# Parts of the k and q weights, made in the MLP and kept in memory, in a two-layer S5 and stick-breaking-attention decoder

## The chip, the cores and the metric

The kernel runs on one core of one Trainium2 chip. The metric is the device time of one execution in microseconds (us): the median of three runs of the kernel before is 2406.37 us (2405.84 to 2408.62). Besides these, one execution was taken with the hardware profiler; all rows below come from it.

## The reference

The model takes x of 1024 tokens by 1024 channels, in fp32. The part that matters here, in short:

```
x1 = LN(2^.5 * x  + S5_mixer(x) @ w_out)
h  = relu(x1 @ w1 + b1)^2               # MLP of layer 0, 4096 wide: first product
x2 = LN(2^.5 * x1 + h @ w2 + b2)        # second product
k, v = split(x2 @ w_kv);  q = x2 @ w_q  # 16 heads of 64
z[t,s] = q_t . k_s / 8,  s < t only
w[t,s] = sigmoid(z[t,s]) * prod_{s<j<t} (1 - sigmoid(z[t,j]))
x3 = LN(2^.5 * x2 + (w @ v) @ w_out2);  then the MLP of layer 1
```

## The kernel before

All products are made of three: every fp32 operand is kept as a high part (cast to the type `fp32r`) and a low part (the rest, in the same type), and a product is high x high + high x low + low x high. `split` (L121 to 123) makes the parts: a cast on ScalarE (`act.copy`, L122) and a subtract on VectorE (`dve.tensor_sub`, L123).

The stages stand one behind the other: the S5 layer and its projections to about 460 us; layer 0's first MLP product ("MLP up", `mlp_up`, names `m0...`) from 460 to 789; the second product (`Down`, names `d0...`) to about 1100; V (`VProject`) to 1194; the projections to K and Q and the attention, interleaved, to about 1640; then its output projection and layer 1's MLP.

**MLP up** is a Strassen-like scheme of 7 products per block of 256 hidden channels: 104 steps of one weight tile [128, 2, 512] (high and low) and 12 matmuls each, which accumulate in banks `m0A`, `m0C`, `m0B`. In each step a sum of raw weight tiles (`m0s...`, from the ring `x1ring`, loaded by SP at L843) is split into a slot (`sl`, 8 slots: 4 of pool `wa`, 4 of pool `wb`) two steps ahead of its use; ScalarE copies some banks out (`m0k...`, `keep`, L913), VectorE combines them (`m0h...`), GpSimd stores them to memory (`h_d`). Beside that `Down.ahead` prepares the next stage: 16 residual tiles (`d0ya`), one per five steps, are loaded by SP (L1041), scaled by ScalarE (L1043), given a bias by VectorE (L1044) and stored by SP (L1045). They live in pool `d0pf` with 4 buffers.

**K, Q and attention.** Per pair of heads p, `project_all` makes K and Q: 48 matmuls on each half, with a weight of [1024 x 128] stored as [128, 1024]. Its two halves (c = 0, 1) are loaded raw by SP (`r_k`, `r_q`, 256 KB, L133, a ring of 3 buffers) and split into slots of `wa` (`w_k`, `w_q`), one unit ahead of use; `VProject.run` does the first of them while V's last tiles are multiplied. `Step` is one block of 128 queries of one head: scores `pz` on TensorE, two sigmoids on ScalarE (`qq`, `be`, L1438 and 1439), a causal fill on GpSimd (L1441), a backward running product on VectorE (the scan, L1447) and a product (L1448), transposes on TensorE (`pt`, L1460), split of the transposed weights (`wTh`, `wTl`), the product with V (`po`, L1474), and a store to `o_d` by SP.

A scheduler orders the instructions of each engine from the order of the code and its own estimates; the engines run them in that order, and so does SP with its DMA issues. A tile of a pool is handed out again when its readers are done.

Of the kernel before, what the change touches and what calls it, by code (L numbers as in the profile page):

```python
# [16 lines left out]
P = 128  # L17
# [28 lines left out]
def trunk(ctx, tc, A, out):  # L46
# [32 lines left out]
    h_d = drp.tile([NP, 7, P, HF], F32, name="h_d")  # L79
    v_d = drp.tile([HEADS, KD, P, P], F32R, name="v_d")  # L80
    o_d = drp.tile([2, D, S], F32, name="o_d")

    class Act:

# [727 lines left out]
    def mlp_up(l, xo, y_tiles, w1, nm, ypool, tpool, tag, wb, uside, rest, down):  # L812
# [165 lines left out]
        for i in range(-LA, NSTEPS):  # L978
            if i + LA < NSTEPS:
                p, m = steps[i + LA]  # L980

                if (p, m) == (0, "M3"):
                    ready[0, "M6"] = operand(0, "M6")
                if (p, m) not in ready:
                    ready[p, m] = operand(p, m)
                if m == "M4" and p + 2 < NP:
                    load_raw(p + 2)
            if i < 0:
                continue
            p, m = steps[i]  # L990
            prod(p, m, ready.pop((p, m)))
            if later:
                later.pop(0)()
            if m == "M5" and p < EA:
                after(p, "M2")
            if m == "M4" and p + 1 < EA:
                keep(p + 1, "M1")
            down.ahead(i, NSTEPS, xo.ring)
            if (p, m) == (0, "M3"):
                continue  # L1000
            later += after(p, m)
            if (p, m) == (0, "M6"):
                after(0, "M3")
# [5 lines left out]
    class Down:  # L1009
# [6 lines left out]

        PARTS = ((0, 0), (1, 0), (0, 1), (1, 1))

        def __init__(self, l, nm, xd, wb, last, then=None):
            self.l, self.nm, self.xd, self.wb, self.last, self.then = l, nm, xd, wb, last, then  # L1020
            self.sl = Slots([wa] * 4 + [wb] * 4)
            self.raw, self.hraw, self.ready = {}, {}, {}
            self.st = ExitStack()
            self.units = [(c, m, p) for c in range(NP // CH) for m in self.ORDER for p in range(c * CH, (c + 1) * CH)]
# [6 lines left out]
        def tile(self, pl, nm_, tag):  # L1031
            return pl.tile([P, HF], F32, tag=tag, name=f"{self.nm}{nm_}")

        def ahead(self, i, n, ring):

            q, r = divmod(i - 12, 5)
            if 0 <= q < 16:
                xs = self.xd[tok(q // 2), half(q % 2)]
# [201 lines left out]
    def w1_ahead(l, w1):  # L1240
# [2 lines left out]
            w1.append(load_w(wa, w1_src(l, j // 2, 0, j % 2), f"m{l}1_{j}", HF)[0])  # L1243
        return one

    class VProject:


# [20 lines left out]
        def run(self, psA, trans, lns, sl):  # L1269
# [21 lines left out]
            for t in range(8):  # L1291
                mm(1, t)
                if t == 4:
                    self.wk0 = by_k(load_w(wa, A["w_k"][0], "k0"))


    with ExitStack() as ph:
        with ExitStack() as ph1:
# [47 lines left out]
                rest = proj_ln(ph2, flat(wo), lambda j: wsl.load(rows2(A["w_out"], j, half(1)), f"so1{j}"),  # L1346
                               gg, xo, x_d[0], y_load, A["lnmg"][0], A["lnmb"][0], "so", y_tiles, w1_ahead(0, w1))
            vpr = VProject()
            down = Down(0, "d0", x_d[0], wb, False, vpr)
            mlp_up(0, xo, y_tiles, w1, "m0", yst, bp, "gg", wb, "right", rest, down)  # L1350
        with ExitStack() as ph1:
            x2T = down.run(ph1)
# [17 lines left out]
    with ExitStack() as ph:  # L1370
# [5 lines left out]
        pso = mkpool(ph, "pso", 1, PSUM)  # L1376
        fl = lambda v_: v_.rearrange("p e t -> p (e t)")

        def load_p(nm, p):
            return by_k(load_w(wa, A[f"w_{nm}"][p], f"{nm}{p}"))  # L1380

        def project_all():


            seq = [(nm, p) for p in range(KD) for nm in "kq"]
            nxt = vpr.wk0
            for i, (nm, p) in enumerate(seq):
                w = nxt
                if i + 1 < len(seq):
                    nxt = load_p(*seq[i + 1])  # L1390
                hi, lo = hl = [qt.tile([P, S], F32R, tag=f"{nm}{y}", name=f"{nm}{y}{p}") for y in "hl"]
                for h in range(2):
                    ps = psj.tile([P, HF], F32, tag="j", name=f"pj{nm}{p}{h}")
                    for k in range(KD):
                        dense_fm({h: ps}, w, x2T, [k], (h,))
                        yield
                    split(hi[:, half(h)], lo[:, half(h)], ps)
                prs[p][nm] = hl
                if nm == "q":
                    stack(p, 0)  # L1400
                    yield
# [231 lines left out]
```

## Time and profile before

| | us |
|---|---|
| median of three runs | 2406.37 |
| profiled execution | 2409.81 |
| its span | 2408.1 |
| TensorE busy in the span | 2283.8 (95%) |
| VectorE busy | 1853.5 (77%) |
| ScalarE busy | 1220.4 (51%) |
| GpSimd busy | 409.1 (17%) |
| granted TensorE clock, mean | 0.981 of full |

The span runs from the first to the last instruction in the trace. In the rows PE is TensorE (PEld its weight loads), DVE VectorE, ACT ScalarE, POOL GpSimd, SP the queue that issues most DMAs. A row of a timeline gives the start, the length, the engine, the line, the operation, output<-input with shapes, and in brackets how long the engine had been idle before it and who released it. Idle time of an engine that nobody waits for costs nothing.

### The profile page before, as it was taken

The numbers are of one execution on the slowest core, as the hardware profiler recorded it, in microseconds if no ns is written. First come the engines' busy times: TensorE is split into PE (matmuls) and PEld (weight loads), VectorE is DVE, ScalarE is ACT, GpSimd is POOL, SyncE is SP. The second block draws the span as 40 slices with busy tenths as digits, with TensorE's granted clock in tenths as the row PEclk, the third lists the DMA queues.
The fourth block names the chain that finished last, engine by engine and source line by source line (L and its number), as shares of the span: only waits on it lengthen the run. The fifth ranks groups of instructions, "written<-read, shape, count | busy, mean of one in ns | idle before, by whom it ended". The sixth has DMA issues, their size and how long they took to land.

```text
span 2408.1 us, 32696 instructions
## 1 busy us (share of the span) xinstructions
PE 2283.8 (95%) x11072; PEld 1873.7 (78%) x11072; DVE 1853.5 (77%) x2899; ACT 1220.4 (51%) x2299; POOL 409.1 (17%) x704
## 2 busy tenths in 40 slices
PE   9987899999999999999999999888989999999996
PEld 7777787777888788888887888766777888788885
DVE  7899674886665787789169999896887666687888
ACT  5455441465555444445156777663356555444443
POOL 4000140012111000001144434341002111100001
PEclk9998999999999999999999999999999999999998
DMA  4221232376444845437655554555457343665432
GB/s 147 61 78 47 60 111 66 136 257 206 145 144 149 303 134 154 148 97 192 123 134 117 129 122 109 119 140 192 139 173 280 147 152 145 228 201 167 135 110 105
DMA packets 195160, 349.38 MB, mean 145 GB/s; under 512 B 23216, under 2 KB 66224, under 8 KB 194992
## 3 DMA queue, kind: packets, MB, share of 16 engines
q1 hardware_dynamic: 136112, 246.61, 32.4%
q0 software_dynamic: 58880, 100.69, 15.1%
q8 instruction: 87, 1.43, 0.3%
q14 instruction: 81, 0.66, 0.1%
HBM read 212.96 MB, written 100.66 MB: 130 GB/s over the span
## 4 chain that ended last, share of the span: by engine, by line
PE 65%; DVE 16%; issue 9%; DMA 4%; ACT 3%; POOL 2%; SPq 0%; POOLq 0%; DVEq 0%; ACTq 0%
PE d0M L1096 4%; PE d0M L1097 4%; PE d0M L1098 4%; PE d1M L1096 4%; PE d1M L1098 4%; PE d1M L1097 4%; DVE qq L1447 2%; PE m0A L832 2%; PE m0A L833 2%; PE m0A L834 2%; PE m1A L832 2%; PE m1A L834 2%; PE m1A L833 2%; DVE be L1448 2%; PE po L1474 2%
## 5 line engine op out<-in xcount | busy, mean ns | idle before, releaser
L1447 DVE TENSOR_TENSOR_SCAN qq<-qq 128x128 f32<-128x128 f32 (+7 forms) x128 | 173.7, 1359 | 12.1 <-POOL qq L1441 11.9
L1096 PE MATMUL d1M<-w_d12M,w_d1HM 128*128 128x512 f32 x448 | 175.7, 393 | 3.9 <-DVE d1y L1105 3.9
L1098 PE MATMUL d1M<-w_d12M,w_d1HM 128*128 128x512 f32 x448 | 175.9, 393 | 0.0
L1096 PE MATMUL d0M<-w_d02M,w_d0HM 128*128 128x512 f32 x448 | 174.7, 391 | 1.2 <-DVE d0y L1105 1.2
L1097 PE MATMUL d1M<-w_d12M,w_d1HM 128*128 128x512 f32 x448 | 175.4, 392 | 0.0
L1097 PE MATMUL d0M<-w_d02M,w_d0HM 128*128 128x512 f32 x448 | 174.8, 390 | 0.0
L1098 PE MATMUL d0M<-w_d02M,w_d0HM 128*128 128x512 f32 x448 | 174.6, 390 | 0.0
L122 ACT CAST w_d1HM<-d1hM 128x512 fp32r<-128x512 f32 x110 | 68.3, 621 | 170.1 <-PE d1M L1098 148.1
L122 ACT CAST w_d0HM<-d0hM 128x512 fp32r<-128x512 f32 x110 | 68.3, 621 | 169.0 <-PE d0M L1098 142.8
L122 ACT CAST wTh<-pt 128x512 fp32r<-128x512 f32 (+1 forms) x192 | 88.1, 486 | 84.1 <-PE pt L1460 83.6
L1460 PE MATMUL pt<-ident,be 128*128 128x128 f32 x576 | 91.2, 283 | 36.4 <-DVE wTl L123 28.0
L192 POOL TENSOR_TENSOR rsd<-ved,nhalf 128x1 f32<-128x1 f32 x16 | 16.2, 1014 | 621.1 <-DVE ved L190 612.9
L1460 PEld LDWEIGHTS pt<-ident,be 128*128 128x128 f32 x576 | 70.3, 144 | 62.1 <-issue 17.8
L123 DVE TENSOR_TENSOR w_d1HM<-d1hM,w_d1HM 128x512 fp32r<-128x512 f32 x110 | 75.8, 689 | 52.3 <-ACT w_d1HM L122 52.2
L123 DVE TENSOR_TENSOR w_d0HM<-d0hM,w_d0HM 128x512 fp32r<-128x512 f32 x110 | 75.9, 690 | 51.5 <-ACT w_d0HM L122 51.4
L123 DVE TENSOR_TENSOR wTl<-pt,wTh 128x512 fp32r<-128x512 f32 (+1 forms) x192 | 99.7, 545 | 11.5 <-ACT wTh L122 11.4
L1448 DVE TENSOR_TENSOR be<-be,qq 128x127 f32<-128x127 f32 (+7 forms) x128 | 99.4, 777 | 7.2 <-POOL be L1441 0.5
L1096 PEld LDWEIGHTS d1M<-w_d12M,w_d1HM 128*128 128x128 f32 x448 | 84.4, 188 | 24.1 <-ACT w_d12M L122 4.3
L1438 ACT ACTIVATE qq<-pz 128x512 f32<-128x512 f32 (+1 forms) x192 | 97.2, 507 | 10.9 <-DVE be L1448 5.3
L1096 PEld LDWEIGHTS d0M<-w_d02M,w_d0HM 128*128 128x128 f32 x448 | 84.1, 188 | 21.2 <-DVE d0y L1105 2.5
L1098 PEld LDWEIGHTS d1M<-w_d12M,w_d1HM 128*128 128x128 f32 x448 | 84.6, 189 | 18.4
L1097 PEld LDWEIGHTS d1M<-w_d12M,w_d1HM 128*128 128x128 f32 x448 | 84.6, 189 | 17.9
(480 smaller groups left out, 7084.5 us busy)
## 6 DMA issues: line engine op xcount, KB each, us to landing
d0hM<-h_d SPq DMA_DIRECT2D x110, 256.0 KB, 2.7
d1hM<-h_d SPq DMA_DIRECT2D x110, 256.0 KB, 2.7
x1ring<-in_w SPq DMA_DIRECT2D x70, 256.0 KB, 3.1
x3ring<-in_w SPq DMA_DIRECT2D x70, 256.0 KB, 3.2
h_d<-m0hs POOLq DMA_DIRECT2D x64, 256.0 KB, 2.8
h_d<-m1hs POOLq DMA_DIRECT2D x64, 256.0 KB, 2.8
d0r<-in_w SPq DMA_DIRECT2D x58, 256.0 KB, 3.7
d1r<-in_w SPq DMA_DIRECT2D x58, 256.0 KB, 3.3
```

Of the source, the lines that this page charges most:

```text
L122: act.copy(hi, src)
L123: dve.tensor_sub(lo, src, hi)
L832: pe.matmul(ps_, wh, xh[:, k], start=first and k == 0, stop=False, skip_group_check=True)
L833: pe.matmul(ps_, wh, xl[:, k], start=False, stop=False, skip_group_check=True)
L834: pe.matmul(ps_, wl, xh[:, k], start=False, stop=k == 3, skip_group_check=True)
L1096: pe.matmul(ps_, hh[:, tok(t)], wh, start=first, stop=False, skip_group_check=True)
L1097: pe.matmul(ps_, hh[:, tok(t)], wl, start=False, stop=False, skip_group_check=True)
L1098: pe.matmul(ps_, hl[:, tok(t)], wh, start=False, stop=last, skip_group_check=True)
L1438: act.activation(qq[:, s0:s1], pz, AF.Sigmoid, scale=-0.125)
L1447: dve.tensor_tensor_scan(out=rev, data0=rev, data1=rev, initial=1.0, op0=ALU.mult, op1=ALU.bypass)
L1448: dve.tensor_mul(be[:, 0:ns - 1], be[:, 0:ns - 1], qq[:, 1:ns])
L1460: pe.transpose(pt[:, b_], self.be[:, tok(s0 + b_)], ident)
```

## The change

A class `SplitKQ` is given to layer 0's `Down` and called in each step of MLP up. It loads each half of each w_k and w_q (32 raw tiles of 256 KB, two per five steps from step 12 on) into a buffer of `d0pf`, splits it four steps later into the next slot of MLP up, and stores the slot, 512 KB, to `kq_d` in memory. In V and in the attention `load_kq` loads the parts from there into the slots of `wa`, 512 KB each, without a split. Lines from 80 on move down by 1 to 31.

```diff
--- before.py
+++ after.py
@@ -79,6 +79,7 @@
     h_d = drp.tile([NP, 7, P, HF], F32, name="h_d")
     v_d = drp.tile([HEADS, KD, P, P], F32R, name="v_d")
     o_d = drp.tile([2, D, S], F32, name="o_d")
+    kq_d = drp.tile([2, KD, 2, P, 2, HF], F32, name="kq_d")
 
     class Act:
 
@@ -995,7 +996,7 @@
                 after(p, "M2")
             if m == "M4" and p + 1 < EA:
                 keep(p + 1, "M1")
-            down.ahead(i, NSTEPS, xo.ring)
+            down.ahead(i, NSTEPS, xo.ring, sl)
             if (p, m) == (0, "M3"):
                 continue
             later += after(p, m)
@@ -1016,7 +1017,8 @@
 
         PARTS = ((0, 0), (1, 0), (0, 1), (1, 1))
 
-        def __init__(self, l, nm, xd, wb, last, then=None):
+        def __init__(self, l, nm, xd, wb, last, then=None, job=None):
+            self.job = job
             self.l, self.nm, self.xd, self.wb, self.last, self.then = l, nm, xd, wb, last, then
             self.sl = Slots([wa] * 4 + [wb] * 4)
             self.raw, self.hraw, self.ready = {}, {}, {}
@@ -1031,8 +1033,10 @@
         def tile(self, pl, nm_, tag):
             return pl.tile([P, HF], F32, tag=tag, name=f"{self.nm}{nm_}")
 
-        def ahead(self, i, n, ring):
-
+        def ahead(self, i, n, ring, sl):
+
+            if self.job:
+                self.job.step(i, self.pf, sl)
             q, r = divmod(i - 12, 5)
             if 0 <= q < 16:
                 xs = self.xd[tok(q // 2), half(q % 2)]
@@ -1243,6 +1247,33 @@
             w1.append(load_w(wa, w1_src(l, j // 2, 0, j % 2), f"m{l}1_{j}", HF)[0])
         return one
 
+    class SplitKQ:
+
+
+        PARTS = [(y, p, c) for p in range(KD) for y in range(2) for c in range(2)]
+
+        def __init__(self):
+            self.raw = {}
+
+        def step(self, i, pl, sl):
+            for j, (y, p, c) in enumerate(self.PARTS):
+                i0 = 12 + 5 * j // 2
+                if i == i0:
+                    self.raw[j] = pl.tile([P, HF], F32, tag="p", name=f"kq{j}")
+                    dma.dma_start(self.raw[j], A[("w_k", "w_q")[y]][p][:, half(c)])
+                elif i == i0 + 4:
+                    t = sl.next().tile([P, 2, HF], F32R, tag="w", name=f"w_kq{j}")
+                    split(t[:, 0], t[:, 1], self.raw.pop(j))
+                    dma.dma_start(kq_d[y, p, c], t.bitcast(F32))
+
+    def load_kq(nm, p):
+        out = []
+        for c in range(2):
+            t = wa.tile([P, 2, HF], F32R, tag="w", name=f"w_{nm}{p}{c}")
+            dma.dma_start(t.bitcast(F32), kq_d["kq".index(nm), p, c])
+            out.append((t[:, 0], t[:, 1]))
+        return by_k(out)
+
     class VProject:
 
 
@@ -1291,7 +1322,7 @@
             for t in range(8):
                 mm(1, t)
                 if t == 4:
-                    self.wk0 = by_k(load_w(wa, A["w_k"][0], "k0"))
+                    self.wk0 = load_kq("k", 0)
 
 
     with ExitStack() as ph:
@@ -1346,7 +1377,7 @@
                 rest = proj_ln(ph2, flat(wo), lambda j: wsl.load(rows2(A["w_out"], j, half(1)), f"so1{j}"),
                                gg, xo, x_d[0], y_load, A["lnmg"][0], A["lnmb"][0], "so", y_tiles, w1_ahead(0, w1))
             vpr = VProject()
-            down = Down(0, "d0", x_d[0], wb, False, vpr)
+            down = Down(0, "d0", x_d[0], wb, False, vpr, SplitKQ())
             mlp_up(0, xo, y_tiles, w1, "m0", yst, bp, "gg", wb, "right", rest, down)
         with ExitStack() as ph1:
             x2T = down.run(ph1)
@@ -1376,9 +1407,6 @@
         pso = mkpool(ph, "pso", 1, PSUM)
         fl = lambda v_: v_.rearrange("p e t -> p (e t)")
 
-        def load_p(nm, p):
-            return by_k(load_w(wa, A[f"w_{nm}"][p], f"{nm}{p}"))
-
         def project_all():
 
 
@@ -1387,7 +1415,7 @@
             for i, (nm, p) in enumerate(seq):
                 w = nxt
                 if i + 1 < len(seq):
-                    nxt = load_p(*seq[i + 1])
+                    nxt = load_kq(*seq[i + 1])
                 hi, lo = hl = [qt.tile([P, S], F32R, tag=f"{nm}{y}", name=f"{nm}{y}{p}") for y in "hl"]
                 for h in range(2):
                     ps = psj.tile([P, HF], F32, tag="j", name=f"pj{nm}{p}{h}")
```

What the scheduler makes of it. First VectorE in MLP up, some 40 us into the stage. `d0ya` are the residual tiles, `w_m01M` the split weights, `m0s` and `m0h` sums of weights and of results. Before:

```order
L1044 TENSOR_TENSOR d0ya_4585<-d0ya_4585,d0b_4254 128x512
L1044 TENSOR_TENSOR d0ya_4714<-d0ya_4714,d0b_4254 128x512
L123 TENSOR_TENSOR w_m01M_4422<-m0sM_4420,w_m01M_4422 128x512
L1044 TENSOR_TENSOR d0ya_4833<-d0ya_4833,d0b_4254 128x512
L123 TENSOR_TENSOR w_m01M_4442<-x1ring,w_m01M_4442 128x512
L901 TENSOR_TENSOR m0sM_4465<-x1ring 128x512
L1044 TENSOR_TENSOR d0ya_4952<-d0ya_4952,d0b_4254 128x512
L929 TENSOR_TENSOR m0hA_4337<-m0kM_4335,m0C_4279 128x512
L123 TENSOR_TENSOR w_m01M_4467<-m0sM_4465,w_m01M_4467 128x512
L929 TENSOR_TENSOR m0hA_4358<-m0kM_4297,m0A_3972 128x512
```

Now, from the same place, and then some 30 rows on:

```order
L1048 TENSOR_TENSOR d0ya_4588<-d0ya_4588,d0b_4255 128x512
L124 TENSOR_TENSOR w_m01M_4423<-m0sM_4421,w_m01M_4423 128x512
L902 TENSOR_TENSOR m0sM_4466<-x1ring 128x512
L124 TENSOR_TENSOR w_m01M_4443<-x1ring,w_m01M_4443 128x512
L930 TENSOR_TENSOR m0hA_4338<-m0kM_4336,m0C_4280 128x512
L124 TENSOR_TENSOR w_m01M_4468<-m0sM_4466,w_m01M_4468 128x512
L930 TENSOR_TENSOR m0hA_4359<-m0kM_4298,m0A_3973 128x512
L1048 TENSOR_TENSOR d0ya_4725<-d0ya_4725,d0b_4255 128x512
```

```order
L902 TENSOR_TENSOR m0sM_4755<-x1ring 128x512
L124 TENSOR_TENSOR w_m01M_4680<-m0sM_4678,w_m01M_4680 128x512
L904 SCALAR_TENSOR_TENSOR m0sM_4781<-m0sM_4755,x1ring 128x512
L124 TENSOR_TENSOR w_kq_4698<-kq_4586,w_kq_4698 128x512
L930 TENSOR_TENSOR m0hA_4590<-m0kM_4565,m0C_4519 128x512
L124 TENSOR_TENSOR w_m01M_4596<-m0sM_4594,w_m01M_4596 128x512
L906 TENSOR_TENSOR m0sM_4810<-x1ring,m0sM_4781 128x512
L930 TENSOR_TENSOR m0hA_4611<-m0kM_4543,m0A_4125 128x512
```

Before, four residual tiles stand among these ten rows (13 of the 16 among 45); now two stand here, and the other 14 come in the rest of the stage, one in some five steps. The first split of a k weight (`w_kq`) comes in the second piece. The same holds for ScalarE and for SP's loads and stores of these tiles.

Then SP where V ends and K begins (`r_v` raw V weights, `x_d` a store of the stage before, `r_k` and `r_q` raw weights of K and Q). Before:

```order
L1259 DMA r_v_9849<-in_w_kv 128x512
L206 DMA x_d<-d0y_6753 128x1024
L1259 DMA r_v_9883<-in_w_kv 128x512
L206 DMA x_d<-d0y_6754 128x512
L133 DMA r_k_10034<-in_w_k 128x512
L206 DMA x_d<-d0y_6754 128x512
L133 DMA r_k_10039<-in_w_k 128x512
L133 DMA r_q_10165<-in_w_q 128x512
L133 DMA r_q_10170<-in_w_q 128x512
L133 DMA r_k_10231<-in_w_k 128x512
L133 DMA r_k_10236<-in_w_k 128x512
```

Now (`r_ao` are raw weights of the attention's output projection, `w_k` and `w_q` slots):

```order
L1290 DMA r_v_10076<-in_w_kv 128x512
L207 DMA x_d<-d0y_6947 128x512
L134 DMA r_ao_15173<-in_sb_out 128x512
L207 DMA x_d<-d0y_6947 128x512
L134 DMA r_ao_15178<-in_sb_out 128x512
L1273 DMA w_k_10226<-kq_d 128x1024
L1273 DMA w_k_10228<-kq_d 128x1024
L1273 DMA w_q_10351<-kq_d 128x1024
L1273 DMA w_q_10353<-kq_d 128x1024
L1273 DMA w_k_10411<-kq_d 128x1024
L1273 DMA w_k_10413<-kq_d 128x1024
```

The raw loads are gone from here; the loads of parts write into the slots themselves, and two loads of the output projection's weights stand ahead of them.

Last VectorE in the attention, in the step of the fourth pair of heads from the rows of the trace below. Before:

```order
L1447 SCALAR_TENSOR_TENSOR qq_2_12759<-qq_2_12759 128x384
L123 TENSOR_TENSOR wTl_0_12775<-pt_00_12776,wTh_0_12774 128x128
L1448 TENSOR_TENSOR be_2_12758<-be_2_12758,qq_2_12759 128x383
L123 TENSOR_TENSOR ql_12495<-pjq_12650,qh_12494 128x512
L123 TENSOR_TENSOR w_q_12853<-r_q_12854,w_q_12853 128x512
L123 TENSOR_TENSOR wTl_0_12775<-pt_10_12825,wTh_0_12774 128x2x128
L1447 SCALAR_TENSOR_TENSOR qq_3_12802<-qq_3_12802 128x512
L1448 TENSOR_TENSOR be_3_12801<-be_3_12801,qq_3_12802 128x511
```

Now:

```order
L1475 SCALAR_TENSOR_TENSOR qq_2_12886<-qq_2_12886 128x384
L124 TENSOR_TENSOR wTl_0_12902<-pt_00_12903,wTh_0_12901 128x128
L1476 TENSOR_TENSOR be_2_12885<-be_2_12885,qq_2_12886 128x383
L124 TENSOR_TENSOR ql_12622<-pjq_12777,qh_12621 128x512
L124 TENSOR_TENSOR wTl_0_12902<-pt_10_12952,wTh_0_12901 128x2x128
L1475 SCALAR_TENSOR_TENSOR qq_3_12929<-qq_3_12929 128x512
L1476 TENSOR_TENSOR be_3_12928<-be_3_12928,qq_3_12929 128x511
```

The subtract of `w_q` is gone, the rest keeps its order; this is so at all 24 places of the attention's steps. TensorE's and GpSimd's orders in the attention are the same as before.

## Rows read from the trace of the kernel before

**Rows 1.** Busy time by stretch (start:end, length, engines with instructions, TensorE clock, DMA share, GB/s).

```profile
450.00:790.00 340.00, 332.77 (x1455) 266.46 (x1454) 234.96 (x365) 198.18 (x335) 59.52 (x110) 0.99 0.53 182
490.00:520.00 30.00, 29.11 (x125) 22.80 (x124) 25.55 (x43) 21.54 (x39) 4.51 (x8) 1.00 0.80 280
520.00:550.00 30.00, 27.70 (x112) 21.87 (x112) 24.30 (x40) 20.01 (x36) 7.52 (x14) 0.94 0.89 304
580.00:610.00 30.00, 30.00 (x130) 24.16 (x129) 18.43 (x28) 16.85 (x28) 3.78 (x7) 1.00 0.33 114
1190.00:1200.00 10.00, 10.00 (x45) 8.05 (x44) 3.20 (x5) 2.58 (x5) 2.63 (x3) 1.00 0.96 220
1300.00:1400.00 100.00, 94.95 (x562) 81.00 (x562) 92.63 (x122) 70.61 (x171) 40.05 (x86) 0.98 0.52 117
1400.00:1500.00 100.00, 94.62 (x569) 80.67 (x568) 92.53 (x125) 69.72 (x169) 42.31 (x90) 1.00 0.56 126
```

**Rows 2.** TensorE waits from 490 to 790: line, releaser, total us, times, longest us.

```profile
PE m0A L832 <- ACT m0kM L913: 2.3, 1, 2.3
PE m0A L832 <- ACT w_m01M L122: 0.9, 1, 0.9
PE m0A L832 <- DVE m0hA L929: 0.7, 1, 0.7
```

**Rows 3.** TensorE waits, attention, 1185 to 1577.

```profile
PE pt L1460 <- DVE wTl L123: 19.5, 20, 2.8
```

**Rows 4.** Splits of w_k: duration ns min/median/max, first and last start us, forms.

```profile
L122 ACT CAST w_k<-r_k x16: 621/624/680, 1189.2 to 1489.6; 128x512 fp32r<-128x512 f32 x16
L123 DVE TENSOR_TENSOR w_k<-r_k,w_k x16: 660/682/693, 1189.8 to 1491.5; 128x512 fp32r<-128x512 f32 x16
```

**Rows 5.** VectorE in order of time, attention (start, length, instruction, [idle before, releaser]).

```profile
1405.41 0.66 DVE L123 TENSOR_TENSOR w_q<-r_q,w_q 128x512 fp32r<-128x512 f32 x1
...
1407.66 0.78 DVE L1447 TENSOR_TENSOR_SCAN qq<-qq 128x256 f32<-128x256 f32 x1 [0.33 <-POOL qq L1441]
...
1412.22 0.68 DVE L123 TENSOR_TENSOR w_q<-r_q,w_q 128x512 fp32r<-128x512 f32 x1
1413.41 0.43 DVE L123 TENSOR_TENSOR wTl<-pt,wTh 128x256 fp32r<-128x256 f32 x1 [0.51 <-ACT wTh L122]
...
1421.39 0.68 DVE L123 TENSOR_TENSOR wTl<-pt,wTh 128x512 fp32r<-128x512 f32 x1
```

**Rows 6.** TensorE in order of time, attention.

```profile
1422.22 0.30 PE L1460 MATMUL pt<-ident,be 128*128 128x128 f32 x1 [1.26 <-DVE wTl L123]
```

**Rows 7.** All engines in order of time where K begins.

```profile
1189.17 1.32 ACT L122 CAST w_k<-r_k 128x512 fp32r<-128x512 f32 x2
...
1193.88 0.40 PE L108 MATMUL pjk<-d0xo_h,w_k 128*128 128x512 f32 x1
```

**Rows 8.** Transfers: issues by line, KB each, median us to landing.

```profile
x1ring<-in_w SPq DMA_DIRECT2D x70, 256.0 KB, 3.1
v_d<-vt POOLq DMA_DIRECT2D x16, 512.0 KB, 4.1
v<-v_d POOLq DMA_DIRECT2D x16, 512.0 KB, 5.3
```

**Rows 9.** All engines in order of time, MLP up, 508 to 534.

```profile
508.74 0.63 ACT L1043 ACTIVATE d0ya<-d0ya 128x512 f32<-128x512 f32 x1 [0.91 <-DMA d0ya<-xm_d]
509.93 0.50 PE L832 MATMUL m0A<-x1T,w_m01M 128*128 128x512 f32 x1 [0.89 <-ACT w_m01M L122]
...
530.42 0.63 ACT L1043 ACTIVATE d0ya<-d0ya 128x512 f32<-128x512 f32 x1 [2.31 <-DMA d0ya<-xm_d]
531.48 1.05 ACT L913 COPY m0kM<-m0A 128x512 f32<-128x512 f32 x2
532.10 0.50 PE L832 MATMUL m0A<-x1T,w_m01M 128*128 128x512 f32 x1 [2.30 <-ACT m0kM L913]
...
533.79 0.63 PE L832 MATMUL m0A<-x1T,w_m01M 128*128 128x512 f32 x1
```

**Rows 10.** The residual tiles d0ya: waits of their lines, and landing times.

```profile
  DMA d0ya<-xm_d: 12.9, 7
...
DMA to landing us min/median/max: 2.5/4.2/6.0
```

## The prediction

> **What bounds the kernel now.** I read the time by stretches first, because the change takes work from one stage (the attention) and gives it to another (the first product of layer 0's MLP). [rows 1] gives busy microseconds of each engine per stretch. The reader should see two things. In the MLP stage TensorE is busy 332.8 of 340 us, and in a typical 30 us of it (580 to 610) all 30.00, while VectorE has 18.4 and ScalarE 16.9: there TensorE is the only limit and the two others have 11 to 13 us spare in each 30. In the attention TensorE is still at 95%, but VectorE stands at 92.5 to 92.6 of 100 us: two engines near their limit, of which either may set the pace.
>
> Then I asked what TensorE waited for. In the MLP stage there are three waits, all before 550, 3.9 us together [rows 2]. In the attention there are 20 waits of TensorE for VectorE's `wTl` (the low part of the transposed weights), 19.5 us in all [rows 3]. So the most that this change can win is in sight: some 4 us plus what a half-speed clock adds in the MLP stage, and 19.5 us in the attention.
>
> **The part taken out of the attention.** 32 pieces of w_k and w_q (16 each) lose one ScalarE cast of 624 ns and one VectorE subtract of 682 ns [rows 4], those of w_q the same within 2 ns: 32 x 0.682 = 21.8 us of VectorE, 32 x 0.624 = 20.0 us of ScalarE. Eight of the 32 lie between 1189 and 1218, where VectorE has 3.2 us of work in the 10 from 1190 [rows 1], so they cost nothing before and save nothing. Of the other 24, in six pairs of heads with four each, I followed where the saved time goes. [rows 5] shows two. The subtract of `w_q` at 1412.22 (0.68 us) is followed at once by 0.51 us in which VectorE waits for ScalarE's `wTh`, and that cast waited for TensorE's transposes: with the subtract gone VectorE only waits longer. The run that TensorE then waits for goes from 1413.41 to the `wTl` at 1421.39, holds no weight split, and is what ends TensorE's 1.26 us wait at 1422.22 [rows 5, 6]. That wait stays whole. The subtract at 1405.41 (0.66 us) is of the second kind: VectorE stands idle for 0.33 us behind it (the scan at 1407.66 waits for GpSimd), so 0.33 us goes into that idle time and at most 0.33 us reaches TensorE. One in four is of this kind. Six pairs times 0.33 us gives 2.0 us. The bounds are 0 and the whole 19.5 us of [rows 3]; I take **-2.0**, as that comes from the pieces themselves.
>
> **What stands in its place there.** The loads of the parts are twice as long (512 KB for 256 KB; 8 MB more over the stage), and SP, which issues in order, now waits at each of them for TensorE to release the weight buffer instead of for VectorE's split. Behind such a load stand stores of the attention's output (`o_d`) and loads of `ol`. A late one costs at most what the longest wait of [rows 3] shows, 2.8 us; it is zero if the buffers are free early, as they were for the splits. Between 0 and +2.8 I take +0.3, near the lower end, since DMA has half its time free in that stage (shares 0.52 and 0.56) [rows 1].
>
> **The hand-over from V to K.** Before, the raw `w_k` was in memory early and only the split had to wait for the buffer: casts at 1189.17, TensorE's first use at 1193.88, no gap [rows 7]. Now the load itself needs the buffer, so it can't start before about 1189.2, and 4.7 us later it is needed. It shares the DMA with the V transfers, share 0.96 there [rows 1]. The nearest transfers of 512 KB take 4.1 us (`v_d<-vt`) and 5.3 us (`v<-v_d`) [rows 8]: first use at 1193.3 to 1194.5, so a loss of 0 to 0.6 us for the first half, and with two to four such loads in the queue at once up to 3. I take **+0.7**. The Trainium skill ("DMA: Bandwidth & Descriptors", section "Anatomy of one DMA") prices a transfer at about 2.0 us plus its bytes at 436 GB/s, an estimate of 3.2 us for 512 KB; by it this term would be zero and the sum 0.7 us lower; the measured 4.1 us at this load is above it, and I go by the row.
>
> **The MLP stage, removed.** The order shows that 14 of the 16 `d0ya` steps (load of a residual tile, scaling on ScalarE, bias on VectorE, store) leave the burst that they formed at 473 to 549 and are spread over the stage, because the raw k and q tiles now take the buffers of their pool. That burst is what makes two of the three waits. ScalarE is in order; at 530.42 it had waited 2.31 us for a `d0ya` load, so its copy `m0kM` came at 531.48, and TensorE lost 2.30 us at 532.10; behind it eight matmuls ran at the lower clock, 0.63 us long and 0.43 us apart instead of 0.23, which is 8 x 0.2 = 1.6 us. In the same way 0.91 us of ScalarE at 508.74 became 0.89 us of TensorE at 509.93 [rows 9]. 2.3 + 1.6 + 0.9 = 4.8 us. It can be 0 (some other burst at the same place) or 5.9 (with the third wait, 0.7, and the refills); I take **-4.8**.
>
> **The MLP stage, added.** 32 raw loads of 256 KB, 32 casts, 32 subtracts, 32 stores of 512 KB, in about 236 us. Cover: 21.8 us of VectorE and 20.0 us of ScalarE per 236 us is 2.8 and 2.5 us in each 30, where 11.6 and 13.2 are idle [rows 1]. If that cover were gone they would cost up to 20 us. DMA: 24 MB in 236 us is 102 GB/s on top of 114; the sum is under the 280 to 304 that the burst moved. The real danger is ScalarE again: 14 `d0ya` and 32 casts stand in order in front of copies that release TensorE's accumulation banks. In the burst 16 such loads made 7 waits of ScalarE, 12.9 us in all [rows 10], and 3.2 us of it came through to TensorE, a quarter. They landed in 4.2 us (median) [rows 10]; ring loads over the stage in 3.1 [rows 8], so a wait of 1.84 us shrinks to 0.74. 46 operations x 7/16 x 0.74 us x 1/4 = 3.7 us if all are issued as late as in the burst; 0 if early enough. The casts are issued four steps (11 us) after their loads by the code, though the scheduler may pull them forward. I take the middle, **+2.0**; the bounds are 0 and, with the burst's landing time kept up for all of the stage, 46 x 7/16 x 1.84 x 1/4 = 9.3.
>
> **The sum.** -2.0 + 0.3 + 0.7 - 4.8 + 2.0 = **-3.8 us**. The profiled execution took 2409.81 us, so 2406.0 against it. The median of the runs shown is 3.4 us lower than the profiled one; the terms are differences, so I take them from the median: 2406.37 - 3.8 = **2402.6 us**. That is 0.16% and, the bound of what can be told from no change being 0.2% (4.8 us), "the same" is its likeliest reading.
>
> **Rivals.**
> - *VectorE was the pace-maker of the attention.* For it: 92.5% busy and every one of the 20 waits ends on VectorE. Against it: three in four splits are followed by idle time of VectorE before the next wait of TensorE. If all waits went, 19.5 us would be won instead of 2.0: 2402.6 - 17.5 = 2385. If half: about 2395. It decides if the idle time behind the splits belongs to chains that VectorE itself had delayed one round earlier. Chance 0.17.
> - *The loads come late in the MLP stage* (slower than before). One mechanism: ScalarE stands in order behind a `d0ya` or a raw tile not yet landed, and TensorE then waits for `m0kM`. With the burst's landing time all through the stage the term is +9.3 instead of +2.0, and the burst's gain may be kept: 2402.6 + 7.3 = 2410; with the half-clock stretches that followed the longest wait, two of them 3 us more, 2413. It decides when the loads of 580 to 780 land in 4.2 us or more (3.1 before). Against it: an idle third of VectorE and ScalarE. The Trainium skill ("DMA: Bandwidth & Descriptors", section "Latency and other measured facts") speaks for it: access to HBM goes from 0.2 us to 2 us at high load, and this stage now carries about twice its traffic; the trace agrees so far as loads took 4.2 us in the burst and 3.1 otherwise. Chance 0.21.
> - *The burst does not go, or another takes its place, and the rest cancels*: +1.0, 2407. This lies within the forecast's own range.
>
> **Chances and range.** Forecast 0.62, with its own range 2397 to 2408 (the burst term 0 to 5.9, the new stalls 0 to 3.7); about a third of it lies below 2401.6 (faster by over 0.2%), the rest is the same. VectorE 0.17: 0.15 faster, 0.02 same. Late loads 0.21: 0.15 slower (above 2411.2), 0.06 same; of the forecast's own 0.42 of "the same", 0.03 go to slower, for a hand-over from V to K at its upper end with no gain elsewhere. Faster 0.20 + 0.15 = 0.35; slower 0.15 + 0.03 = 0.18; the same 0.39 + 0.02 + 0.06 = 0.47. The range that holds 8 in 10 leaves out the full form of the first rival and the worst of the second: 2393 to 2413.
>
> **What the profile after would show.** Right: no wait of TensorE for `m0kM` near 532 and no low clock there; `d0ya` of 500 to 740 in small pieces; VectorE about 21 us and ScalarE about 20 us less from 1190 to 1520 and as much more from 520 to 760, where TensorE stays at 30.00 of 30; 17 to 18 us of waits for `wTl` left; a gap under 1 us before the first K matmul. Wrong: waits for `wTl` under 12 us (first rival), or several new waits for `m0kM` between 560 and 780 with loads over 4 us (second rival), or a gap of over 2 us at the first K or Q matmul.

## The result and the profile after

The changed kernel takes 2419.71 us (median of 6 runs, 2417.99 to 2422.30) against 2406.70 us (6 runs) beside it: 13 us or 0.65% slower (ratio 1.0065, 95% interval 1.0053 to 1.0077). I had predicted 2402.6 us with a range of 2393 to 2413: wrong in size and in sign. Its profiled execution took 2418.55 us.

**Where it went, by stage.** Each stage runs from its first matmul to the first of the next, MLP up from its first matmul into `m0C` (492.0 before, 489.0 after; some into `m0A` and `m0B` come earlier), the attention from the first scores to the last `po`. One profiled execution each (us):

| | MLP up | second product | V | K to first scores | attention |
|---|---|---|---|---|---|
| before | 297.5 | 309.0 | 95.4 | 28.8 | 430.2 |
| after | 305.0 | 308.5 | 95.1 | 30.2 | 433.6 |
| 13 kernels below that load and split raw weights in the attention | | | | 28.8 to 29.1 | 424.7 to 429.6 |

The 430.2 of the first row is the highest of its kind; the median of the 13 others is 426.6. So MLP up costs 7.5 us in this pair of profiles, the start of the attention 1.4, the attention 3.4 to 7. Both halves of the change lose. (The two profiled executions are only 8.7 us apart, partly because the changed kernel's began the stage 3.0 us earlier; over all kernels here this start lies between 486.6 and 493.2, so I count that as chance.)

Busy time by stretch, as [rows 1]:

```profile
450.00:790.00 340.00, 327.46 (x1413) 260.69 (x1412) 243.89 (x386) 207.97 (x361) 58.05 (x107) 0.98 0.72 250
580.00:780.00 200.00, 193.06 (x812) 153.83 (x812) 133.00 (x208) 122.44 (x211) 37.84 (x70) 0.98 0.78 271
1300.00:1400.00 100.00, 92.94 (x556) 79.66 (x555) 86.23 (x114) 63.35 (x157) 41.01 (x88) 0.98 0.60 147
1400.00:1500.00 100.00, 92.18 (x559) 78.85 (x557) 88.09 (x115) 63.58 (x155) 41.60 (x87) 1.00 0.58 141
```

In MLP up TensorE now idles 7 of the 200 us from 580 to 780, where it had idled none; VectorE and ScalarE are at 67% and 61% there, so they are not the bound by their work. In the attention VectorE fell from 92.5 to 88 and 86 of 100, as worked out, and yet TensorE is busy 2 us less in each 100.

TensorE's waits from 490 to 794, as [rows 2], and ScalarE's waits for DMA in the same stretch (total us, times, longest us):

```profile
PE m0A L833 <- DVE m0hA L930: 4.2, 3, 2.7
PE m0A L833 <- ACT m0kM L914: 2.8, 2, 2.6
PE m0C L833 <- ACT m0kM L914: 1.7, 1, 1.7
```

```profile
ACT w_m01M L123 <- DMA kq_d<-w_kq: 31.8, 16, 4.3
ACT d0ya L1047 <- DMA d0ya<-xm_d: 5.4, 5, 2.3
ACT w_kq L123 <- DMA kq_d<-w_kq: 3.1, 3, 1.4
```

The first row of ScalarE is new and names a thing that the prediction never priced: a cast of an ordinary MLP weight (`w_m01M`) waits for the *store* of a k or q part. The parts are split into the ring of 8 weight slots, and a slot is not free until its store, 512 KB, has landed (4.3 us, median). All engines of one such wait, in order of time:

```profile
677.57 0.62 ACT L123 CAST w_m01M<-m0sM 128x512 fp32r<-128x512 f32 x1 [3.17 <-DMA kq_d<-w_kq]
...
680.26 0.62 ACT L123 CAST w_m01M<-m0sM 128x512 fp32r<-128x512 f32 x1 [2.07 <-DMA kq_d<-w_kq]
680.78 0.58 ACT L914 COPY m0kM<-m0A 128x512 f32<-128x512 f32 x1
...
681.41 0.50 PE L833 MATMUL m0A<-x1T,w_m01M 128*128 128x512 f32 x1 [2.57 <-ACT m0kM L914]
```

Two casts stand 3.17 and 2.07 us at slots that stores hold; the copy `m0kM`, which frees TensorE's bank, is behind them, and TensorE loses 2.57 us. The wait of 1.65 at 656 has the same chain. The third large one, 2.72 at 750, comes through VectorE: it stood 1.90 us at a late load of the ring (744.50) and then 1.28 us for a cast that ScalarE, 4.34 us at a slot held by a store, had begun late:

```profile
747.02 0.62 ACT L123 CAST w_m01M<-m0sM 128x512 fp32r<-128x512 f32 x1 [4.34 <-DMA kq_d<-w_kq]
747.67 0.69 DVE L124 TENSOR_TENSOR w_m01M<-m0sM,w_m01M 128x512 fp32r<-128x512 f32 x1 [1.28 <-ACT w_m01M L123]
...
750.34 0.51 PE L833 MATMUL m0A<-x1T,w_m01M 128*128 128x512 f32 x1 [2.72 <-DVE m0hA L930]
```

Behind each of the two longest waits eight matmuls run 0.61 to 0.63 us long (the last of the first eight 0.58) and some 0.43 apart instead of 0.23, from 682.92 and from 751.14, at the lower of TensorE's two clock levels (the granted clock is 0.94 of full in 670 to 700 and in 730 to 760). That is some 3.2 us, an estimate of 16 x 0.2; the kernel before had one such stretch, at 533.

```profile
682.92 0.63 PE L833 MATMUL m0A<-x1T,w_m01M 128*128 128x512 f32 x1
```

TensorE's waits in the attention, 1189 to 1586, as [rows 3]:

```profile
PE pt L1488 <- DVE wTl L124: 21.7, 19, 2.9
PE pt L1488 <- POOL be L1469: 3.3, 6, 0.6
PE pz L1464 <- DMA qs<-qh: 1.3, 1, 1.3
```

19.5 us became 21.7; waits for GpSimd are 3.3 us (0.3 before), and one for a transfer of q is new. The waits repeat per pair of heads, and the pair shows what is new: 51.78 us before (1344.73 to 1396.51), 52.44 after (1351.88 to 1404.32). `kls<-kl` below is the DMA, issued by GpSimd, that copies a head's low part of K to where its scores read it. Before, all engines in order of time, in the K half of a pair:

```profile
1378.18 0.52 POOL L1410 DMA_DIRECT2D kls<-kl  x1
...
1379.02 0.67 DVE L123 TENSOR_TENSOR w_k<-r_k,w_k 128x512 fp32r<-128x512 f32 x1
...
1379.71 0.33 SPq L133 DMA_DIRECT2D r_q<-in_w_q  x1
...
1381.11 0.69 DVE L123 TENSOR_TENSOR kl<-pjk,kh 128x512 fp32r<-128x512 f32 x1
```

After, the same place:

```profile
1384.16 0.33 SPq L1273 DMA_DIRECT2D w_k<-kq_d  x1
...
1385.34 0.52 POOL L1438 DMA_DIRECT2D kls<-kl  x1
...
1389.23 0.69 DVE L124 TENSOR_TENSOR kl<-pjk,kh 128x512 fp32r<-128x512 f32 x1 [1.12 <-issue]
...
1391.80 0.30 PE L1488 MATMUL pt<-ident,be 128*128 128x128 f32 x1 [0.56 <-DVE wTl L124]
```

`kl` overwrites the K of the pair before, so it must wait until the transfer `kls<-kl` has read it. Before, the raw load came out 1.5 us after that transfer was issued (1378.18), released by VectorE's split. Now the load of parts is released by TensorE's last use of the slot and goes out 1.2 us *ahead* of it. That `kls` takes 3.8 us to land instead of 2.8, `kl` waits 1.12 us (the profile names no releaser; the landing, 1389.1, fits), `wTl` behind it is late, and TensorE has a wait of 0.56 that was not there. Over all pairs, before and after:

```profile
kls<-kl POOLq DMA_DIRECT2D x32, 256.0 KB, 2.9
kls<-kl POOLq DMA_DIRECT2D x32, 256.0 KB, 4.0
```

Each head has two such transfers. From 1270 to 1520 the second of each head, ten in all, has a load of parts 0.5 to 1.2 us ahead of it in the changed kernel and takes 3.8 to 5.1 us; before, with no load ahead, nine of the ten take 2.8 to 3.0. The first of each head has no load of weights in the 3 us ahead of it in either kernel and stays within 0.6 us of before. The tenth of before, issued at 1429.95, takes 4.4 us and makes the same wait: `kl` waits 1.75 us, TensorE 1.19, and that pair takes 53.20 us, a part of the high 430.2.

### The profile page after: what moved, and what is told of

It is laid out like the page before. It is cut to its first block, busy times and chain, and to the rows that moved or that the text cites. A ratio compares the mean times of both kernels' runs of the same rounds, so it can differ in the third digit from the quotient of the medians.

```text
span 2416.8 us, 32789 instructions
## 1 busy us (share of the span) xinstructions
PE 2280.3 (94%) x11072; PEld 1867.3 (77%) x11072; DVE 1849.9 (77%) x2899; ACT 1218.3 (50%) x2299; POOL 408.9 (17%) x704
## 4 chain that ended last, share of the span: by engine, by line
PE 53%; DVE 16%; issue 15%; DMA 7%; POOL 4%; ACT 3%; SPq 0%; POOLq 0%; DVEq 0%; ACTq 0%
PE d0M L1100 4%; PE d0M L1101 4%; PE d0M L1102 4%; PE d1M L1100 4%; PE d1M L1102 4%; PE d1M L1101 4%; DVE qq L1475 2%; DMA kq_d<-w_kq 2%; POOL h_d L927 2%; PE po L1502 2%; DVE be L1476 2%; PE pt L1488 2%; PE pg L109 1%; PE m0A L833 1%; PE pg L111 1%
## 5 line engine op out<-in xcount | busy, mean ns | idle before, releaser
L1488 PE MATMUL pt<-ident,be 128*128 128x128 f32 x576 | 91.3, 283 | 40.1 <-DVE wTl L124 29.3
```

The source lines that it names most:

```text
L1488: pe.transpose(pt[:, b_], self.be[:, tok(s0 + b_)], ident)
```

## The experiments

Baselines drift by 1 to 3 us between batches, so ratios are to the kernel before on the same chip. All kernels start from the changed one unless the text says otherwise; the edits are shown shortened.

**e1, the MLP part alone.** `load_kq` loads and splits raw weights again.

```
-    load_kq: 2 x dma(w_, kq_d[...])
+    load_kq: by_k(load_w(wa, A[f"w_{nm}"][p], ...))
```

> The MLP part of the change alone: the k and q weights are loaded, split and stored as parts during MLP up, but V and the attention load the raw weights and split them as before (the stored parts are not read). My theory now: the change lost in two places, 7.5 us inside MLP up (297.5 to 305.0 us from the first m0C matmul to the first d0M matmul), because a slot of the weight ring stays taken until the 512 KB store from it has landed and ScalarE, in order, stands at the next cast into that slot; and 4.8 us between the first K matmul and the last po matmul. By it this kernel keeps 305 us in MLP up and ScalarE's 32 us of waits on the stores, has pairs of heads of 51.8 us again, and takes 2406.7 + 7.5 - 3.0 (earlier start of the stage) = 2411 us, 2409 to 2414. Rival: the whole loss is made in the attention or by what the stage leaves behind (then 2403 to 2407); other rival: all of it is in MLP up (then 2418 to 2421).

1.0023 (1.0010 to 1.0036), MLP up 302.4 us, pairs 51.78, ScalarE 36.1 us at stores. The loss has two parts. MLP up was 2.6 us shorter than I said: its code is that of the changed kernel, but no matmul of it ran at the lower clock in this profile, where the changed kernel's has the 16 above.

**e2, the attention part alone.**

```
-    PARTS = [... for p in range(KD) ...];  kq_d["kq".index(nm), p, c]
+    PARTS = [... for p in range(1) ...] at steps 60 + 5 * j;  kq_d["kq".index(nm), 0, c]
```

> The attention part alone: in MLP up only the four parts of the first pair of heads are split and stored (at steps 60 to 79), and every later load of parts in V and the attention reads these four again, 512 KB each and without a split (so the output uses the first pair's weights everywhere). My theory: the attention loses 4 to 5 us by itself, pairs of heads take 52.4 us instead of 51.8, VectorE's kl waits for the kls transfers; MLP up within 1.5 us of before; in all 2409 to 2413 us. Rival: the attention loses only because of the MLP part (2404 to 2408); second rival, my prediction's: the relief of VectorE wins 2 us or more (under 2405).

1.0036 (1.0021 to 1.0050), pairs 52.46 us, attention 433.6 us. As my theory said; my prediction's relief of VectorE did not show.

**e7, half the load.** e2, with only the high part loaded and used twice.

```
-    dma(t, kq_d[...]); out (t[:, 0], t[:, 1])
+    dma(t[:, 0], kq_d[...][:, 0]); out (t[:, 0], t[:, 0])
```

> As e2_attn_512, but each load brings only the high part, 256 KB, as the raw loads of before, and it is used for both parts (so the products leave the low parts out). What is left of the change in the attention is the missing split and the place of the wait. My theory, that the longer loads collide with the kls transfers: pairs of heads go back to 51.8 us or under, kls lands in 2.9 us (median), K0 to the end of the attention 457 us or less, 2402 to 2406 us in all. Rival, that the missing subtracts move VectorE onto kl before the kls transfers have landed, whatever the loads: pairs stay at 52.4 us, VectorE's kl waits stay at 5 to 6 us, 2409 to 2412 us.

1.0006 (0.9994 to 1.0019), but pairs 52.4 us, `kls` 3.8 us, attention 432.0: my theory on the *length* of the load fell. A load half as long, at the same moment, makes nearly the same wait; the length adds to the start, K to first scores (28.7 us here, 30.6 in e2). No run moved the load back; that its moment decides rests on the order of the rows above and on this run.

**e8, a second buffer for kl**, in the whole change.

```
-    kl = qt.tile(tag="kl")
+    kl = ap_.tile(tag="kx") if p % 2 else qt.tile(tag="kl")
```

> The whole change, with two buffers for the low part of K (even and odd pairs of heads), so that kl need not wait until the kls transfers of the pair before have read it. If VectorE's wait at kl is what makes pairs of heads 0.66 us longer, they go back to 51.8 us or lower and the attention gets 4 us shorter than in the changed kernel: ratio to before 1.003 to 1.005 (2412 to 2416). Rival: the wait moves to kh or to the q tiles, or was never what TensorE waits for: the ratio stays at 1.006 to 1.007.

1.0031 (1.0020 to 1.0041), attention 426.6 us, pairs 51.78 us. `kls` still lands in 4.0 us, but nobody waits for it: that wait had cost the attention 7.0 us (433.6 - 426.6; e2 and e10 below, 433.6 - 426.7). TensorE, in order of time, one pair:

```profile
1353.11 0.30 PE L1489 MATMUL pt<-ident,be 128*128 128x128 f32 x1 [0.56 <-DVE wTl L124]
1366.33 0.30 PE L1489 MATMUL pt<-ident,be 128*128 128x128 f32 x1 [0.61 <-POOL be L1470]
1378.84 0.30 PE L1489 MATMUL pt<-ident,be 128*128 128x128 f32 x1 [1.27 <-DVE wTl L124]
1404.89 0.30 PE L1489 MATMUL pt<-ident,be 128*128 128x128 f32 x1 [0.56 <-DVE wTl L124]
```

The wait in the K half is gone. The wait of 0.27 to 0.29 at the second place before is 0.61 here and now ends on GpSimd: TensorE comes there 0.3 us earlier, waits 0.3 us longer, and the pair is not a bit shorter.

**e10 and e11, what the relief is worth, and a control.** e2 with that buffer, and the kernel before with that buffer.

> e2_attn_512 with the two buffers of e8_kl_two: the attention without splits, without the MLP cost and without the wait at kl; so the most that taking the splits out can win here (the output uses the first pair's weights everywhere). My theory now, that the relief of VectorE and ScalarE is worth nothing to TensorE: pairs of heads 51.6 to 51.8 us, K0 30 us, ratio to before 0.999 to 1.002. Rival, the relief wins once the wait is gone (2 us or more, as I had predicted): ratio 0.999 or lower, pairs under 51.4 us.

> The kernel before with two buffers for the low part of K, nothing else: the control of e8. As kl did not wait there, no difference: ratio 0.999 to 1.001, pairs of heads 51.8 us. If it is faster by 0.2% or more, e8 shows a gain of its own and not the cause of the loss.

1.0005 (0.9995 to 1.0015) and 0.9998 (0.9989 to 1.0008). e10's attention takes 426.7 us and its pairs 51.78, as with the splits in: taking them out of the attention is worth nothing that these runs can tell, and the buffer has no gain of its own.

**e3, no stores.** e1 without `dma(kq_d[y, p, c], t)`.

> As e1_job_only, but the split parts are not stored (so 32 raw loads, 32 casts, 32 subtracts stay, and a slot is free as soon as VectorE has written it). Slot theory: MLP up goes back to 297 to 299 us, no wait of ScalarE for stores, 2403 to 2406 us. Rival, load on ScalarE and VectorE or late raw and d0ya loads: MLP up stays at 303 to 305 us, 2410 to 2412 us.

0.9990 (0.9977 to 1.0004), MLP up 296.3 us. So 32 loads, casts and subtracts cost nothing; the stores do. But ScalarE stood 22.6 us at `d0ya` loads, which I had taken for cured by spreading them.

**e4 to e6, e9, e12: the stores, made elsewhere.**

```
e4  split into tiles of d0pf (5 buffers), low part over the raw tile; 2 x 256 KB
e5  e1, dve.tensor_copy(src[:, 0:1], t[:, 1, 0:1]); 2 x dma(kq_d[...], src)
e6  e1, t = js.tile(...)   # js: one buffer; 7 h tiles for 8
e9  e1, 2 x dma(kq_d[...], raw)   # d0pf 5 buffers
e12 e5, copy and stores issued by GpSimd
```

> The whole change, but the parts are made outside the weight ring: the high part in a tile of the pool of the raw tiles (5 buffers instead of 4), the low part over the raw tile, and two stores of 256 KB. Slot theory: the same bytes are stored, and MLP up takes 297 to 300 us; the attention stays as in the changed kernel; 2411 to 2414 us. Rival, traffic: the same bytes move, so MLP up stays near 305 us and the time at 2418 to 2421 us.

> As e1_job_only (raw loads and splits in the attention), with the same 16 MB of stores in MLP up at the same places, but the stores read a tile of their own (512 columns, stored twice, of which one column is copied from the split, so the stored values are not the parts); the slot of the ring is free once the split is done. Slot theory: MLP up takes 296 to 298.5 us as in e3_no_store (296.3), where e1_job_only took 302.4; ScalarE has under 5 us of waits on stores; 2399 to 2404 us where the kernel before takes 2403.8. Rival, traffic (the stores slow the loads of raw weights and of d0ya, or fill the write side of memory): 301 to 305 us of MLP up, 2407 to 2411 us.

> As e1_job_only, with the parts split into one buffer of their own (4 KB in each partition; the h tiles of MLP up get 7 buffers instead of 8 to make room) and stored from there, so no slot of the weight ring waits for a store, but the next split of parts does. Slot theory in its wide form (any ScalarE cast that waits for a store landing blocks what stands behind it): the waits stay, now at the casts of parts, MLP up 299 to 304 us. Slot theory in its narrow form (only the ring of 8 matters): 296 to 299 us. Rival, traffic: 302 us or more.

> As e1_job_only (raw loads and splits in the attention), with the same 16 MB of stores spread over MLP up, but they read the raw tile (twice 256 KB, so the stored values are not the parts) in a pool of 5 buffers instead of 4, so no ScalarE or VectorE instruction waits for a store to land, only SP's next raw load does. Theory (an engine that runs in order stands at a store): MLP up takes 295 to 299.5 us, near e3_no_store's 296.3, ScalarE's and VectorE's waits on stores are gone, 2400 to 2405 us where the kernel before takes about 2404. Rival, traffic by itself: 302 to 308 us of MLP up and 2407 to 2413 us. Second rival, SP stands at the stores and the ring loads come late: VectorE waits for the ring by more than 10 us.

> As e5_traffic, with GpSimd, which has little to do in MLP up, making the one-column copy and issuing the stores (so the stored values are not the parts): 16 MB of stores, while no ScalarE or VectorE instruction waits for a store of parts and SP does not issue them. Attention raw and split as before. Theory (an in-order engine on TensorE's path stands at a store): MLP up 296 to 299.5 us, 2400 to 2405 us where the kernel before takes about 2404.5. Rival, traffic by itself (ring and d0ya loads land late): MLP up 302 us or more, 2407 us or more, with ScalarE's waits on d0ya or VectorE's on the ring over 20 us.

My theory's numbers missed in all five (the rival "traffic" came true in number in e6 and e12): MLP up 323.2, 308.0, 315.5, 312.5 and 319.2 us; ratios 1.0128, 1.0027, 1.0052, 1.0055 and 1.0057. In none was the waiting gone. In four an engine stood at the new place that a store held: ScalarE's cast of the high part (18.7 us), VectorE's copy (19.8), ScalarE's cast of parts (21.6), GpSimd's copy (63.8, e12). In e9 SP, in order, stood 51.6 us at raw tiles that had not landed yet, ahead of their stores, and ScalarE 29.3 us at `d0ya`. My edits had made new waiters, and tell little on traffic.

**e13, traffic that holds no buffer.** e3 plus 30 times `dma(kq_d[...], h_d[b, q:q + 2])`, 512 KB each (30 in the trace; the 22 that I expected is a miscount).

> e3_no_store (296.3 us of MLP up) plus 22 copies of 512 KB inside memory, from blocks of h_d stored some steps earlier to kq_d, spread over MLP up: 11 MB read and 11 MB written more (the changed kernel's stores write 16 MB). No buffer in the chip's own memory is held by them, nobody reads their result, and only SP issues them. Theory (TensorE loses where an in-order engine stands at a buffer that a store still holds): MLP up stays at 296 to 299 us, 2400 to 2405 us where the kernel before takes about 2404.5. Rival, traffic by itself: 302 us or more, 2407 us or more, with d0ya or ring loads landing in 4 us or more.

1.0062 (1.0045 to 1.0079), MLP up 313.6 us: my theory in its narrow form (only held buffers matter) fell. Ring loads land in 4.9 us, and ScalarE stands 41.6 us at `d0ya`.

**e14, e15, e18: the same traffic without d0ya.** e13, e9 and e1 with

```
-            if 0 <= q < 16:
+            if 0 <= q < 16 and not self.job:   # no d0ya steps in layer 0
```

> e13_dram_copies without the 16 d0ya steps (load, scaling, bias, store of the residual left out, so the output lacks the scaling and the bias): the same copies inside memory, but no ScalarE instruction in MLP up that waits for a freshly issued small load. If the traffic costs time only where ScalarE, in order, stands at a late d0ya load, MLP up falls from 313.6 to 300 us or less and the time to 2405 or less. If traffic costs time by itself (ring loads late, VectorE at the ring), MLP up stays over 305 us.

> e9_store_raw without the 16 d0ya steps: 16 MB of stores that no ScalarE or VectorE instruction waits for, and no d0ya. Same question: 300 us or less of MLP up (e9: 312.5) if the in-order stand at d0ya carries the loss; over 305 us if the traffic does.

> e1_job_only (the change's slots and stores in MLP up, raw weights in the attention) without the 16 d0ya steps (so the output lacks the scaling and the bias of the residual). The pair to e15, which has the same bytes and no d0ya either, but no slot that a store holds (291.4 us of MLP up). If the slot held by a store costs time by itself, MLP up takes 296 us or more here and ScalarE keeps 20 us or more of waits on stores; if a store's hold is harmless without d0ya, 291 to 294 us.

294.8, 291.4 and 298.1 us of MLP up; ratios 0.9972 (0.9960 to 0.9984), 0.9962 (0.9946 to 0.9978) and 0.9991 (0.9982 to 1.0001). Stretch 580 to 780 of e14, e15 and e18, and ScalarE's waits for DMA in e18:

```profile
580.00:780.00 200.00, 200.00 (x859) 160.89 (x858) 133.73 (x203) 125.00 (x208) 37.74 (x70) 1.00 0.66 229
```

```profile
580.00:780.00 200.00, 200.00 (x859) 160.85 (x858) 134.16 (x204) 125.54 (x210) 37.76 (x70) 1.00 0.67 230
```

```profile
580.00:780.00 200.00, 196.08 (x835) 155.57 (x834) 129.62 (x200) 118.55 (x203) 37.87 (x70) 1.00 0.70 245
```

```profile
ACT w_m01M L123 <- DMA kq_d<-w_kq: 41.5, 19, 4.0
ACT w_kq L123 <- DMA kq_d<-w_kq: 3.9, 2, 3.0
```

In e14 and e15 TensorE is busy 200.00 of these 200 us at 229 and 230 GB/s, with all casts and subtracts, and in e15 it waits nowhere from 493 to 785. e14 has two waits before 580, 1.77 us at 547 and 1.07 at 567, behind VectorE's 4.00 us at a tile of `h` that a store held and 3.17 at a late load of the ring. So neither the work nor the traffic costs TensorE anything where ScalarE stands at no DMA and VectorE at none for long (e15: 1.9 us at most, at ring loads). With the same bytes, a slot held by a store costs 298.1 - 291.4 = 6.7 us (e18 against e15; the ratios differ by 0.0029, some 7 us), and `d0ya` on top 302.4 - 298.1 = 4.3 us (e1 against e18). None of these three profiles has a matmul at the lower clock. (e15 also has one more buffer of `d0pf`, stores 64 times 256 KB for 32 times 512, and reads the raw tile; no run sets these apart from the held slot.) The stages are of one profile each, so 1 to 3 us of these differences may be chance (e11 has 299.5 where before has 297.5, and e8 305.4, e1 302.4 where the changed kernel has 305.0).

**e16, e17: the burst of d0ya, in the kernel before.** Scaling and bias on GpSimd; and one buffer, so that no burst forms.

```
e16 -  act.activation(yt, Copy, scale=ALPHA); dve.tensor_add(yt, yt, b2)
    +  pool.tensor_scalar_mul(yt, yt, ALPHA); pool.tensor_add(yt, yt, b2)
e17 -  yt from d0pf (4 buffers)
    +  yt from a pool of its own (1 buffer)
```

> The kernel before with the scaling and the bias of d0ya and d1ya on GpSimd instead of ScalarE and VectorE, in both layers, nothing else: what the runs point to, since ScalarE then has no short-lead load to stand at. If the stand at d0ya is what costs in the kernel before too (my prediction's term of 4.8 us), MLP up takes 291 to 295 us instead of 297.5, and the time is 0.1 to 0.3% under before (2398 to 2403). Rival: GpSimd, in order, now stands at these loads and its stores of h come late, so VectorE waits for h tiles: same or slower, 2405 to 2410.

> The kernel before with one buffer of its own for d0ya (and d1ya), so that the 16 steps can't form the burst at 473 to 549 but stand some ten VectorE instructions apart; the work is the same. My prediction's term: without the burst 4.8 us less in MLP up (292 to 294 us), 2400 to 2403 us. Rival, seen in e3 (ScalarE stood 22.6 us at spread d0ya loads): spread loads land late for ScalarE as well, MLP up 296 to 299 us, ratio 0.999 to 1.001.

e16: 1.0176 (1.0161 to 1.0190). GpSimd takes 1.9 and 1.4 us for the two operations, its stores of h come late, and TensorE waits up to 11.6 us. VectorE is slowed as well: from 491 to 570, 20 of its 38 operations on 128x512 tiles that overlap one of GpSimd's take 1.05 to 2.1 us, while 29 of the 30 others take 0.68 or 0.69. So e16 does not tell what relief of ScalarE is worth. e17: 1.0014 (1.0004 to 1.0023), MLP up 298.5 us, ScalarE 19.9 us at `d0ya`: spread in this form is no better than the burst. No version here that computes the whole result beats the kernel before by more than its interval (e3, 0.9990, comes nearest); e14 and e15 do, but they leave the residual's scaling and bias out.

## Why the prediction was wrong, point by point

- *The burst of d0ya, -4.8 us*: failed as a gain of the change. The waits of [rows 9] are gone, as forecast, but others came in their place: a spread `d0ya` load is issued as shortly ahead of ScalarE's scaling as one in the burst (2.8 to 7.4 us; the one of [rows 9] 4.5). e17, spread alone with one buffer, takes 1 us more, which may be chance, not 4.8 less. I took away a wait by name and did not ask whether its cause, the short lead, goes too. That the burst costs something stays likely: e2, e7 and e10, with 9 or 10 of the 16 left at its place instead of 15, take 295.1, 293.6 and 295.9 us, 1.6 to 3.9 less than before. What taking the steps *out* gives, e15's 291.4 us shows.
- *New stalls in MLP up, +2.0, at most 9.3*: the mechanism was the named rival's, ScalarE in order and TensorE at `m0kM`, but at another place. I priced raw loads and `d0ya`, and left out what a split into the ring does to the ring: its slot stays taken until its store has landed. That is the largest piece (6.7 us between e18 and e15). The half-clock stretches that the rival priced at 3 us came too. The two terms together, -2.8 in the sum, measured +7.5.
- *Cover for 21.8 us of VectorE and 20.0 us of ScalarE*: right (e3, e14).
- *Relief of VectorE in the attention, -2.0*: the reading of [rows 5] was right in its main part, that the time saved becomes idle time, and the 2.0 that I kept was too much: 0 (e10, 1.0005, 0.9995 to 1.0015).
- *SP's waits and longer loads there, +0.3*: failed, and cost the attention 3.4 to 7 us; 7.0 by e8 against the changed kernel. I looked for a late load. The load came *early*, released by TensorE instead of VectorE (SP's waits at these loads from 1230 to 1560 all end on TensorE), ahead of `kls`, and `kl` stood behind that.
- *Hand-over from V to K, +0.7*: no gap; from V's first matmul to K's first it is 95.1 us, 95.4 before. The loss came 30 us later, 1.3 us at `qs<-qh`, and only with the long loads (K to first scores 30.1 to 30.7 us; 28.7 with e7's).
- *Skill and row at that term*: the loads of parts landed in 3.7 us (`w_k`) and 4.8 (`w_q`), so the estimate of 3.2 us by the Trainium skill ("DMA: Bandwidth & Descriptors", section "Anatomy of one DMA", which fits it for transfers issued by GpSimd; these go out by SP) was under both, yet its conclusion, no gap at K, was the right one.
- *The rival that VectorE paces the attention* (2385): out, by e10.

The slower rival's time, 2410 to 2413, was for one of two losses, and its condition, loads of 4.2 us or more from 580 to 780, was not met (medians 3.4 for the ring, 3.8 for `d0ya`, 3.9 for the raw parts).

## What to carry to other kernels

Before a tile is written into a ring that feeds the critical path, ask when the slot comes free again: a store out of it holds it until it has landed, and an engine that runs in order puts that time in front of all that it does next. When a transfer's release moves from one engine to another, look for what the transfer now gets in front of. Work taken off an engine that was 92% busy was worth nothing here, because idle time stood between it and the next wait of the bottleneck; the timeline told most of that in advance, the busy share did not.

## What I had not expected of the hardware

MLP up carries 229 GB/s with ring loads landing in 4.7 us (median; 3.1 before) and TensorE at 200.00 of 200 us (e14): longer landings by themselves did not touch it in that stretch (580 to 780). GpSimd takes 1910 ns (median, e16) to scale a 128x512 tile in fp32, where ScalarE takes 632, and beside such work VectorE's 0.68 us operations took up to 2.1 us. The same `kls` transfer that landed in 2.8 to 3.0 us with no load of weights ahead of it (nine of ten) took 3.8 to 5.1 us with one issued 0.5 to 1.2 us ahead.
